# Layer-0 attention: value products grouped by six key tiles, wider maxima with a shift row written by DMA, column-tiled sums

## The chip, the core and the metric

The kernel runs on one core of a Trainium2 chip. Its work is spread over TensorE (PE; its weight loads are shown as PEld), VectorE (DVE), ScalarE (ACT), GpSimd (POOL) and SyncE (SP, which here issues nearly all DMAs). The metric is device time in microseconds of one execution, lower is better; three executions of the kernel before the change took 2945.24, 2954.23 and 2960.78 us.

## The reference

A backbone of two layers over 2048 tokens and 256 context tokens. Layer 0 has a convolution beside a grouped-query attention (8 heads of 64, 2 key heads, keys of context and tokens together, so 2304), layer 1 a Fourier mixing beside a neighbourhood attention. Only the attention of layer 0 is touched by the change:

```python
def dense_attn(q, k, v):
    Bq, Lq, Hq, dh = q.shape
    Hk = k.shape[2]
    qg = q.reshape(Bq, Lq, Hk, Hq // Hk, dh)
    s = jnp.einsum('bqkgd,bskd->bkgqs', qg, k).astype(jnp.float32) * (dh ** -0.5)
    p = jax.nn.softmax(s, axis=-1).astype(v.dtype)
    o = jnp.einsum('bkgqs,bskd->bqkgd', p, v)
    return o.reshape(Bq, Lq, Hq * dh)
...
    y_b = blocked_attn(q, jnp.concatenate([ck, k], axis=1), jnp.concatenate([cv, v], axis=1))
    y_a = conformer_conv(a_val, a_gate, conv_w, conv_b, ln_g, ln_b)
    y = jnp.concatenate([y_a, y_b], axis=-1) * jax.nn.silu(z)
    x = x + gate * (y @ w_out)
    if need_ctx:
        cq = rms_norm(uc[..., AB_Q_OFF:AB_K_OFF].reshape(Bx, L, B_HEADS, HEAD_DIM), qn_g)
        yc_b = dense_attn(cq, ck, cv)
```

For a query the context attends to the 256 context keys only, the tokens to all 2304.

## The kernel before

The stages follow each other: input projection and convolution of layer 0, this attention (`ab_attention`), the output projection of layer 0, then the same for layer 1. In the profiled execution the attention lies between about 735 and 1600 us.

**Units and steps.** The attention works in units: two heads of one group for 256 queries, so 512 query columns. 32 units (token queries) have 18 tiles of 128 keys, 4 units (context queries, put in at indices 0, 4, 8 and 12) have 2. A step of the schedule is one key tile of one unit, 584 in all; `first` is the step at which a unit starts. Scores stand with the keys on partitions. They are negated, and high and low halves of queries and keys are kept apart: a score is two products, `s<-q,k0h` (high and low query on the high keys) and `s<-qm,k0l` (high query on the low keys, with further rows below that carry the shift).

**Maxima, a unit ahead.** So that no exponential overflows, each query's greatest score is taken off. `chunk` (line 854) computes scores again in one pass, with the queries on partitions: five products of up to 512 keys for each of four groups of 128 queries, 16 of 512 keys and 4 of 256 in a unit, each reduced by DVE from one of three PSUM buffers `m` (line 864). `least` joins the five columns, and `shift_row` (line 870) transposes the result on PE, and DVE (line 874) spreads it over four rows of the contraction of `qm`, one for each 128 queries. This is done 7 steps (`AHEAD`) or more ahead of the unit; a chunk falls on each 0.85 of a step.

**Scores, exponentials, values.** `score` (line 881) puts its two products into one of two PSUM buffers `s`; ACT's exponential (line 890) writes `pr`, of which there are six. Every second step, three steps (`LAG`) later, `multiply` (line 893) does the value products of two tiles (line 900): they are plain float32, each with 64 output columns, one in the upper and one in the lower half of the array, so that the two run side by side; the trace records each as two instructions, so a pair of tiles shows as x4. `add` sums the exponentials over the tiles, 7 tiles on DVE (`accd`), 11 on POOL (`accp`).

**A unit's end.** `unload` copies the values out of PSUM on ACT. Then a chain with fixed distances (`CHAIN`) from the last step of the unit: `join` adds both sums on POOL, `sum_high` (ACT) and `sum_low` (DVE) split them, `total` (line 950, tile `row`) sums over the partitions with two products into one row, which ACT copies to `srow` (line 956); SP puts it on 128 partitions (`rc`, line 958), `invert` takes reciprocals on DVE (line 964), two DMAs (lines 965, 967) bring them by way of DRAM to all partitions (`r`); `divide` (POOL, line 971), `fold` (ACT, two copies) and `store` (POOL, line 983, and a DMA) follow. The pool `rp` holds one buffer each of `srow`, `sh`, `sl` and `r`.

**What sets the order.** `at(step, order, f)` notes what each step does; the loop at the end of `ab_attention` emits it step by step, in the order of the second number, under `manual_schedule`, which keeps this order on PE, ACT, DVE and POOL. Each engine works its own list in that order and stands where the next entry isn't ready. The DMAs on SP aren't under that order; the framework's scheduler places them. `extra` puts in the background work by step: the modulation's columns of both layers (`ada_part`, 512 KB loads and small products, up to about step 130), the patterns of layer 1's attention bias (DMAs), and from step 220 the convolution's norm.

## Time and profile before

| | us |
|---|---|
| median of three runs | 2954.23 |
| lowest, highest run | 2945.24, 2960.78 |
| span of the profiled execution, first to last instruction | 2944.6 |
| attention, first score to last value product | 836 |
| PE, DVE, POOL, ACT busy in the whole span | 2764.9, 1855.9, 1531.5, 1134.3 |

The page gives the profiled execution's span, and no time outside it; the span is just under the lowest timed run. An engine's busy time is the union of its instructions' records. The records of PE overlap, since a product drains while the next one streams in, so the time a product costs is read from start to start, not from its length. In a row of the timeline stand start, length, engine, line, operation, output<-inputs, the shape and the count; in brackets the idle time ahead of it and what ended it.

### The profile page before, as it was taken

To read this page: it belongs to the slowest core of one execution; us is meant where nothing else is said; L and a number is where in the kernel's file an instruction comes from. 1 tells how busy PE (TensorE), PEld (TensorE's weight loads), DVE (VectorE), ACT (ScalarE), POOL (GpSimd) and SP (SyncE) were. 2 spreads that over 40 slices of the span, in tenths; PEclk is the share of its full clock that TensorE was granted. 3 is DMA by queue.
4 is the path that set the end of the run, shared out by engine and by line. 5 is a ranking of instruction groups with operands and counts; after the bars stand their busy time and mean duration, and the time that the engine had idled before them with its cause. 6 is when DMAs were issued, how large, how long until landed. Compare 5 with 4: busy or idle time off the path is not lost.

```text
span 2944.6 us, 40977 instructions
## 1 busy us (share of the span) xinstructions
PE 2764.9 (94%) x14481; PEld 2128.3 (72%) x14481; DVE 1855.9 (63%) x2867; ACT 1134.3 (39%) x2103; POOL 1531.5 (52%) x1173
## 2 busy tenths in 40 slices
PE   7988799986999999999999999999999997998998
PEld 5988799886444444444445887988898886888787
DVE  4798869896877788888887564101211336777663
ACT  3223131320354555555554223123222335777421
POOL 3568624846465788778785754222122312455343
PEclk9999899998999999999999999999999998999999
DMA  8224131361642343331123653433333349999852
GB/s 249 91 77 147 53 106 47 96 179 36 196 136 78 123 138 101 90 121 55 51 63 106 235 166 136 150 127 106 126 140 128 111 152 238 220 246 225 273 197 89
DMA packets 345752, 397.66 MB, mean 135 GB/s; under 512 B 54844, under 2 KB 270444, under 8 KB 340555
## 3 DMA queue, kind: packets, MB, share of 16 engines
q1 hardware_dynamic: 344971, 390.85, 44.9%
q10 hardware_dynamic: 576, 4.19, 0.4%
q8 instruction: 114, 1.87, 0.3%
q14 instruction: 91, 0.75, 0.1%
HBM read 270.34 MB, written 129.78 MB: 136 GB/s over the span
## 4 chain that ended last, share of the span: by engine, by line
PE 65%; DMA 11%; DVE 9%; POOL 6%; issue 4%; ACT 1%; SPq 0%; POOLq 0%; ACTq 0%; DVEq 0%
PE av L900 9%; PE s L885 9%; PE mm L415 7%; PE mm L417 7%; PE mm L416 7%; PE m L862 6%; DVE acc L517 5%; DMA nv<-v_d 4%; POOL wlo L431 4%; PE mo L1087 3%; PE mo L1086 3%; PE mo L1085 3%; DMA nk<-k 3%; PE mm L424 2%; PE mm L426 1%
## 5 line engine op out<-in xcount | busy, mean ns | idle before, releaser
L431 POOL TENSOR_TENSOR wlo<-wraw,whi 128x1024 fp32r<-128x1024 f32 x86 | 323.8, 3774 | 499.7 <-ACT whi L430 481.1
L864 DVE TENSOR_REDUCE ast<-m 128x1 f32<-128x512 f32 (+1 forms) x656 | 398.7, 626 | 176.8 <-PE m L862 174.5
L890 ACT ACTIVATE pr<-s 128x512 f32<-128x512 f32 x584 | 343.1, 595 | 298.6 <-PE s L885 253.9
L925 POOL TENSOR_TENSOR accp<-accp,pr 128x512 f32<-128x512 f32 x283 | 398.7, 1409 | 88.1 <-ACT pr L890 74.2
L517 DVE SCALAR_TENSOR_TENSOR acc<-u,cw,acc 128x1151 f32<-128x1151 f32 (+1 forms) x240 | 366.5, 1582 | 0.0
L900 PE MATMUL av<-pr,vt 128*64 128x512 f32 x1168 | 317.4, 622 | 0.0
L417 PE MATMUL mm<-hi_ab,wlo 128*128 128x384 f32 x768 | 260.6, 341 | 39.1 <-POOL wlo L431 39.1
L415 PE MATMUL mm<-hi_ab,whi 128*128 128x384 f32 x768 | 261.0, 346 | 11.6 <-DVE qraw L729 7.2
L416 PE MATMUL mm<-lo_ab,whi 128*128 128x384 f32 x768 | 261.7, 342 | 0.0
L415 PE MATMUL mm<-hi_cd,whi 128*128 128x512 f32 x640 | 250.8, 392 | 1.1 <-ACT hi_cd L379 1.1
L416 PE MATMUL mm<-lo_cd,whi 128*128 128x512 f32 x640 | 250.1, 391 | 0.4 <-DVE lo_cd L380 0.4
L417 PE MATMUL mm<-hi_cd,wlo 128*128 128x512 f32 x640 | 246.7, 390 | 0.0
L417 PEld LDWEIGHTS mm<-hi_ab,wlo 128*128 128x128 f32 x768 | 147.5, 192 | 39.8 <-POOL wlo L431 39.8
L925 DVE TENSOR_TENSOR accd<-accd,pr 128x512 f32<-128x512 f32 x165 | 165.7, 1004 | 0.9 <-ACT pr L890 0.5
L1642 DVE TENSOR_TENSOR nlo<-npt,nhi 128x512 fp32r<-128x512 f32 x192 | 123.6, 644 | 62.1 <-ACT nhi L1640 61.4
L862 PEld LDWEIGHTS m<-k1h,q 128*128 128x128 f32 x328 | 62.2, 190 | 132.9 <-DVE ast L864 84.9
L415 PEld LDWEIGHTS mm<-hi_ab,whi 128*128 128x128 f32 x768 | 147.5, 193 | 14.1 <-DVE qraw L729 7.6
L1604 POOL TENSOR_SCALAR npr<-npr,nst 128x640 f32<-128x640 f32 (+1 forms) x128 | 108.1, 858 | 89.8 <-DVE nst L1603 66.7
L371 DVE TENSOR_SCALAR ht<-ptr,scale,shift 128x384 f32<-128x384 f32 (+2 forms) x96 | 61.2, 671 | 147.4 <-PE ptr L368 146.7
L862 PEld LDWEIGHTS m<-k0h,q 128*128 128x128 f32 x328 | 63.3, 195 | 125.0 <-DVE ast L864 80.6
L430 ACT ACTIVATE whi<-wraw 128x1024 fp32r<-128x1024 f32 x88 | 92.9, 1059 | 148.3 <-PE mm L416 135.5
L416 PEld LDWEIGHTS mm<-lo_ab,whi 128*128 128x128 f32 x768 | 147.8, 193 | 0.8 <-DVE lo_ab L380 0.8
(321 smaller groups left out, 7002.1 us busy)
## 6 DMA issues: line engine op xcount, KB each, us to landing
wraw<-in_cd_w_in_dram SPq DMA_DIRECT2D x46, 512.0 KB, 4.0
wraw<-in_ab_w_in_dram SPq DMA_DIRECT2D x42, 512.0 KB, 3.5
pat_d<-big SPq DMA_DIRECT2D x72, 256.0 KB, 3.7
nk<-k SPq DMA_DIRECT2D x32, 576.0 KB, 12.7
pat<-pat_d SPq DMA_DIRECT2D x24, 768.0 KB, 6.5
nv<-v_d SPq DMA_DIRECT2D x128, 128.0 KB, 7.0
adaraw<-in_ab_w_ada_dram SPq DMA_DIRECT2D x24, 512.0 KB, 6.1
adaraw<-in_cd_w_ada_dram SPq DMA_DIRECT2D x24, 512.0 KB, 3.7
```

What stands on the lines that cost most here:

```text
L415: nc.tensor.matmul(ps, a, hh[:, k, cols], start=k == 0, stop=False)
L416: nc.tensor.matmul(ps, a, hl[:, k, cols], start=False, stop=False)
L417: nc.tensor.matmul(ps, b, hh[:, k, cols], start=False, stop=k == KT - 1)
L431: (eng or nc.vector).tensor_tensor(out=lo, in0=src, in1=hi.bitcast(F32), op=ALU.subtract)
L517: ins = nc.vector.scalar_tensor_tensor(out=acc[:, :n], in0=u[:, tap : tap + n], scalar=cw[:, ch, tap : tap + 1], in1=acc[:, :n], op0=ALU.m ...
L862: nc.tensor.matmul(ps[:, :n], lhs, kt[hp // 2][0][:, a : a + n], start=True, stop=True)
L864: nc.vector.tensor_reduce(out=s["st"][:, qt, col : col + 1], in_=ps[:, :n], axis=AX.X, op=ALU.min)
L885: nc.tensor.matmul(ps[:], kt[hp // 2][key][:, k * P : k * P + P], s[x][:].rearrange("p j n -> p (j n)"), start=key == 0, stop=key == 1,)
L890: nc.scalar.activation(pr[:], ps[:], AF.Exp, scale=-1.0)
L900: nc.tensor.matmul(s["av"][x * 64 : x * 64 + 64], vt[:, k - 1 + x, kv * 64 : kv * 64 + 64], s["pr"][k - 1 + x][:], start=k == 1, stop=k == ...
L925: eng.tensor_tensor(out=s[name][:], in0=first_in[:], in1=s["pr"][k][:], op=ALU.add)
L1642: return lambda: nc.vector.tensor_tensor(out=lo[:, :o], in0=pt[:, :o], in1=hi[:, :o].bitcast(F32), op=ALU.subtract)
```

## The change

- Value products are done in groups of six tiles, at steps 5, 11 and 17 of a unit (a unit of two tiles: at its second step), straight behind that step's score and chunk. `pr` has nine buffers.
- A chunk covers 1024 keys of 128 queries: two products into a PSUM tile of two banks, one reduction by DVE. The last 256 keys of all four groups of queries go together. Nine chunks in a unit, every second step. `m` has two such tiles.
- The shift is one row of the contraction in place of four. DVE negates the maxima into `sr` (queries on partitions), and four DMAs, 128 elements of 4 bytes each, write them into row 64 of `qm`. The transpose and DVE's spreading go.
- `join`, `sum_high` and `sum_low` go. `total` sums `accd` and `accp` by two float32 products in two column halves, into one of the two buffers of `s`, behind the first group of value products that ends at least five steps after the unit. `spread` copies rows 0 to 64 on ACT and sends two rows to `rc`; `invert` adds them before the reciprocal. The last unit sums with full-width float32 products.
- DVE takes the tiles 4, 5, 10, 11, 15, 16, 17, and adds them at the step of their group's value products; POOL's additions come one step after the score, not two.
- The other differences of the diff are comments and docstrings left out.

```diff
-            lo = kp.tile([68, T], F32R, name=f"k{kv}l")
+            lo = kp.tile([65, T], F32R, name=f"k{kv}l")
...
-            tp = self.pool(es, "apt", 6)
+            tp = self.pool(es, "apt", 9)
...
-            ps_m = self.pool(es, "psm", 3, PSUM)
+            ps_m = self.pool(es, "psm", 2, PSUM)
             ps_s = self.pool(es, "pss", 2, PSUM)
             ps_a = self.pool(es, "psa", 1, PSUM)
-            ps_r = self.pool(es, "psr", 1, PSUM)
             ps_c = self.pool(es, "psc", 1, PSUM)
             self.inv_d = [self.dram(f"inv{a}", [1, 512]) for a in range(2)]
-            onesr = rp.tile([P, P], F32R, name="onesr")
-            nc.vector.tensor_copy(onesr[:], self.ones[:])
-            AHEAD, LAG, SUM, RATE, ROW = 7, 3, 2, 0.85, 4
+            AHEAD, SUM, RATE, GROUP = 7, 1, 2, 6
...
-            CHAIN = (5, 7, 9, 11, 14, 19, 21, 22)
+            CHAIN = (1, 4, 9, 11, 12)
...
-            def chunk(i, qt, c):
+            def chunk(i, c):
                 b, hp = units[i]
                 s = state[i]
-                a = c * 512
-                n = min(512, tiles[i] * P - a)
-                lhs = s["q"][:, qt // 2, (qt % 2) * P : (qt % 2) * P + P]
-                ps = ps_m.tile([P, 512], F32, name="m", tag="m")
-                nc.tensor.matmul(ps[:, :n], lhs, kt[hp // 2][0][:, a : a + n], start=True, stop=True)
-                col = c if b else 5
-                nc.vector.tensor_reduce(out=s["st"][:, qt, col : col + 1], in_=ps[:, :n], axis=AX.X, op=ALU.min)
-
-            def least(i):
-                st = state[i]["st"]
-                nc.vector.tensor_reduce(out=st[:, :, 5:6], in_=st[:, :, 0:5], axis=AX.X, op=ALU.min)
+                ps = ps_m.tile([P, 1024], F32, name="m", tag="m")
+                key = kt[hp // 2][0]
+                if b and c < 8:
+                    parts = [(c // 2, c % 2 * 1024 + x * 512, 512) for x in range(2)]
+                else:
+                    parts = [(qt, 2048 if b else 0, 256) for qt in range(4)]
+                for x, (qt, a, n) in enumerate(parts):
+                    lhs = s["q"][:, qt // 2, (qt % 2) * P : (qt % 2) * P + P]
+                    nc.tensor.matmul(ps[:, x * n : x * n + n], lhs, key[:, a : a + n], start=True, stop=True)
+                if len(parts) == 2:
+                    nc.vector.tensor_reduce(
+                        out=s["st"][:, c // 2, c % 2 : c % 2 + 1], in_=ps[:], axis=AX.X, op=ALU.min
+                    )
+                else:
+                    nc.vector.tensor_reduce(
+                        out=s["st"][:, :, 2 if b else 3], in_=ps[:].rearrange("p (q n) -> p q n", q=4), axis=AX.X, op=ALU.min
+                    )
 
             def shift_row(i):
                 s = state[i]
-                pt = ps_r.tile([P, 512], F32, name="row", tag="row")
-                nc.tensor.transpose(pt[0:4, 0:P], s["st"][:, :, 5], self.ident[:])
-                nc.vector.scalar_tensor_tensor(
-                    out=s["qm"][64:68].rearrange("p j (i n) -> p (j i) n", n=P),
-                    in0=pt[0:4, 0:P].unsqueeze(1).broadcast_to((4, 4, P)), scalar=-1.0,
-                    in1=self.ident[0:4, 0:4].unsqueeze(2).broadcast_to((4, 4, P)), op0=ALU.mult, op1=ALU.mult,
-                )
+                st = s["st"]
+                if units[i][0]:
+                    nc.vector.tensor_reduce(out=st[:, :, 3:4], in_=st[:, :, 0:3], axis=AX.X, op=ALU.min)
+                row = sp.tile([P, 4], F32R, name="sr", tag="sr")
+                nc.vector.tensor_scalar(out=row[:], in0=st[:, :, 3], scalar1=-1.0, scalar2=None, op0=ALU.mult)
+                for qt in range(4):
+                    to = s["qm"][64:65, qt // 2, (qt % 2) * P : (qt % 2) * P + P].bitcast(F32)
+                    nc.sync.dma_start(to.rearrange("o (n f) -> o n f", f=1), row[:, qt : qt + 1].bitcast(F32))
...
-            def multiply(i, k):
+            def multiply(i, first_k, n):
                 b, hp = units[i]
                 s = state[i]
-                if k == 1:
+                if first_k == 0:
                     s["av"] = ps_a.tile([P, 512], F32, name="av", tag="av")
                 kv = hp // 2
-                for x in range(2):
+                for k in range(first_k, first_k + n):
+                    x = k % 2
                     nc.tensor.matmul(
-                        s["av"][x * 64 : x * 64 + 64], vt[:, k - 1 + x, kv * 64 : kv * 64 + 64], s["pr"][k - 1 + x][:],
-                        start=k == 1, stop=k == tiles[i] - 1,
+                        s["av"][x * 64 : x * 64 + 64], vt[:, k, kv * 64 : kv * 64 + 64], s["pr"][k][:],
+                        start=k < 2, stop=k >= tiles[i] - 2,
                     )
...
+            def by_dve(i):
+                return [4, 5, 10, 11, 15, 16, 17] if i < len(units) - 1 else list(range(TAIL, NT))
             def add(i, k):
                 s = state[i]
-                n = tiles[i]
-                if n == 2:
-                    mine, eng, name = [0, 1], nc.vector, "accd"
-                else:
-                    dve = [3 * x + 2 for x in range(5)] + [16, 17] if i < len(units) - 1 else list(range(TAIL, n))
-                    mine, eng, name = (dve, nc.vector, "accd") if k in dve else ([x for x in range(n) if x not in dve], nc.gpsimd, "accp")
+                if tiles[i] == 2:
+                    s["accd" if k == 0 else "accp"] = s["pr"][k]
+                    return
+                dve = by_dve(i)
+                mine, eng, name = (dve, nc.vector, "accd") if k in dve else ([x for x in range(NT) if x not in dve], nc.gpsimd, "accp")
...
-            def join(i):
+            def total(i):
                 s = state[i]
-                if "accp" in s:
-                    nc.gpsimd.tensor_tensor(out=s["accd"][:], in0=s["accd"][:], in1=s["accp"][:], op=ALU.add)
-
-            def sum_high(i):
-                s = state[i]
-                s["sh"] = rp.tile([P, 512], F32R, name="sh", tag="sh")
-                nc.scalar.activation(s["sh"][:], s["accd"][:], AF.Copy)
-
-            def sum_low(i):
-                s = state[i]
-                s["sl"] = rp.tile([P, 512], F32R, name="sl", tag="sl")
-                nc.vector.tensor_tensor(
-                    out=s["sl"][:], in0=s["accd"][:], in1=s["sh"][:].bitcast(F32), op=ALU.subtract
-                )
-
-            def total(i):
-                s = state[i]
-                pt = ps_r.tile([P, 512], F32, name="row", tag="row")
-                m = 1 if i < len(units) - 1 else P
-                for x in ("sh", "sl"):
-                    nc.tensor.matmul(pt[0:m], onesr[:, 0:m], s[x][:], start=x == "sh", stop=x == "sl")
-                if m == P:
+                pt = s["tot"] = ps_s.tile([P, 512], F32, name="s", tag="s")
+                if i == len(units) - 1:
+                    for x in ("accp", "accd"):
+                        nc.tensor.matmul(pt[:], self.ones[:], s[x][:], start=x == "accp", stop=x == "accd")
                     s["r"] = rp.tile([P, 512], F32, name="r", tag="r")
                     nc.vector.reciprocal(s["r"][:], pt[:])
                     return
-                row = rp.tile([1, 512], F32, name="srow", tag="srow")
-                nc.scalar.activation(row[:], pt[0:1], AF.Copy)
-                s["rc"] = sp.tile([P, 4], F32, name="rc", tag="rc")
-                nc.sync.dma_start(s["rc"][:], row[0:1].rearrange("o (p f) -> o p f", f=4))
+                for x, name in enumerate(("accd", "accp")):
+                    nc.tensor.matmul(pt[x * 64 : x * 64 + 64], self.ones[:, 0:64], s[name][:], start=True, stop=True)
+            def spread(i):
+                s = state[i]
+                if "r" in s:
+                    return
+                row = rp.tile([65, 512], F32, name="srow", tag="srow")
+                nc.scalar.activation(row[:], s["tot"][0:65], AF.Copy)
+                s["rc"] = sp.tile([P, 2, 4], F32, name="rc", tag="rc")
+                for x in range(2):
+                    nc.sync.dma_start(s["rc"][:, x], row[64 * x : 64 * x + 1].rearrange("o (p f) -> o p f", f=4))
 
             def invert(i):
                 s = state[i]
                 if "r" in s:
                     return
-                nc.vector.reciprocal(s["rc"][:], s["rc"][:])
-                nc.sync.dma_start(self.inv_d[i % 2].rearrange("o (p f) -> (o p) f", f=4), s["rc"][:])
+                rc = s["rc"]
+                nc.vector.tensor_tensor(out=rc[:, 0], in0=rc[:, 0], in1=rc[:, 1], op=ALU.add)
+                nc.vector.reciprocal(rc[:, 0], rc[:, 0])
+                nc.sync.dma_start(self.inv_d[i % 2].rearrange("o (p f) -> (o p) f", f=4), rc[:, 0])
...
-                chunks = [(qt, c) for qt in range(4) for c in range(5 if units[i][0] else 1)]
+                n = 9 if units[i][0] else 1
                 time = min(time - RATE, first[i] - AHEAD)
-                last = int(time // 1)
-                for x in reversed(chunks):
-                    at(int(time // 1), 4, bind(chunk, i, *x))
-                    begin = int(time // 1)
-                    time -= RATE
-                time += RATE
+                last = time
+                for x in reversed(range(n)):
+                    begin = time = last - RATE * (n - 1 - x)
+                    at(time, 3, bind(chunk, i, x))
                 at(begin - 3, 0, bind(load_q, i))
                 at(last - 2, 0, bind(load_high, i))
-                if units[i][0]:
-                    at(last + 1, 5, bind(least, i))
-                at(last + ROW, 1, bind(shift_row, i))
+                at(last, 5, bind(shift_row, i))
+            bursts = [first[i] + k for i, n in enumerate(tiles) for k in range(n) if k % GROUP == GROUP - 1 or k == n - 1]
             for i, n in enumerate(tiles):
                 for k in range(n):
                     s = first[i] + k
                     at(s, 2, bind(score, i, k))
-                    if k % 2 == 1:
-                        at(s + LAG + 0, 3, bind(multiply, i, k))
-                    at(s + SUM, 6, bind(add, i, k))
+                    end = min(k // GROUP * GROUP + GROUP, n)
+                    if k == end - 1:
+                        at(s, 4, bind(multiply, i, k // GROUP * GROUP, end - k // GROUP * GROUP))
+                    late = k in by_dve(i) and i < len(units) - 1
+                    at(first[i] + end - 1 if late else s + SUM, 6, bind(add, i, k))
                 e = first[i] + n - 1
-                at(e + LAG, 4, bind(unload, i))
-                ds = {len(units) - 2: CHAIN[:5] + (22, 24, 25), len(units) - 1: (2, 4, 4, 8, 8, 9, 10, 11)}.get(i, CHAIN)
-                for d, f in zip(ds, (join, sum_high, sum_low, total, invert, divide, fold, store)):
-                    at(e + d, 7, bind(f, i))
+                at(e + 1, 1, bind(unload, i))
+                t = min([x for x in bursts if x >= e + 5], default=e + 2)
+                at(t, 7, bind(total, i))
+                ds = CHAIN if i < len(units) - 1 else (0, 0, 1, 2, 3)
+                for d, f in zip(ds, (spread, invert, divide, fold, store)):
+                    at(t + d, 8 if t + d == t else 1, bind(f, i))
```

8 lines of the change are left out of this document (4 added, 4 removed).

## The prediction

> **What bounds the kernel now.** I read the page's head first, then the chain that ended last, then the stretch of the attention.
>
> ```profile
> span 2944.6 us, 40977 instructions
> ...
> PE 2764.9 (94%) x14481; PEld 2128.3 (72%) x14481; DVE 1855.9 (63%) x2867; ACT 1134.3 (39%) x2103; POOL 1531.5 (52%) x1173
> ...
> PE 65%; DMA 11%; DVE 9%; POOL 6%; issue 4%; ACT 1%; SPq 0%; POOLq 0%; ACTq 0%; DVEq 0%
> ```
>
> PE leads. The busy times of the stretch from the first score to the last value product:
>
> ```profile
> 752.00:1588.00 836.00, 819.20 (x3403) 388.25 (x3403) 674.76 (x1033) 447.56 (x803) 617.49 (x474) 0.99 0.33 97
> ```
>
> The columns after the length are PE, PEld, DVE, ACT, POOL, granted clock, DMA share. 836 us carry 584 steps (one key tile each: 32 units of 18, 4 units of 2), 1.43 us a step, and PE is busy in 98%. A busy PE may still lose time between its products, so the PE timeline decides; the time of a product is the distance to the next start:
>
> ```profile
> 937.65 0.40 PE L862 MATMUL m<-k0h,q 128*128 128x512 f32 x1
> 937.89 0.40 PE L885 MATMUL s<-q,k0h 128*128 128x512 f32 x1
> 938.12 0.40 PE L885 MATMUL s<-qm,k0l 68*128 68x512 f32 x1
> 938.45 1.08 PE L900 MATMUL av<-pr,vt 128*64 128x512 f32 x4
> 939.46 0.49 PE L862 MATMUL m<-k0h,q 128*128 128x512 f32 x1
> 939.80 0.40 PE L950 MATMUL row<-sh,onesr 128*1 128x512 f32 x1
> 940.03 0.39 PE L950 MATMUL row<-sl,onesr 128*1 128x512 f32 x1
> ```
>
> A score or maximum product costs 0.23 (937.65 to 937.89). The one ahead of the value products takes 0.33 and the one behind them 0.34: the change of kind costs 0.10 on each side. The value products of two tiles take 1.01 between. So a pair alone costs 1.21 us, and there is no gap to blame: the attention is bound by PE's own queue. Near the end the trace has two pairs together:
>
> ```profile
> 1585.48 0.39 PE L885 MATMUL s<-qm,k1l 68*128 68x512 f32 x1
> 1585.80 1.94 PE L900 MATMUL av<-pr,vt 128*64 128x512 f32 x8
> 1587.66 0.49 PE L1121 MATMUL pl<-mean_w,sm 128*128 128x1 f32 x3
> ```
>
> 1.86 us for both: the second pair costs 0.85 where a lone one costs 1.21.
>
> **The change part by part.** *Bursts.* A unit of 18 tiles goes from nine lone pairs to three bursts of three: 1.21 + 2 x 0.85 = 2.91 instead of 3.63, 0.72 a burst, 96 bursts: **-69**. This rests on one place; were a later pair 1.01, only the edges went: 192 x 0.20 = -38.
>
> *Sums.* Before: two products in fp32r, 0.23 each. After: two fp32 column tiles behind a burst, as one more value pair, 0.85. 35 x (0.85 - 0.46): **+14**. Join (POOL), high (ACT) and low (DVE) part go, with PE's wait for them:
>
> ```profile
> PEld row L950 <- DVE sl L940: 11.6, 8, 3.3
> ...
> PE row L950 <- DVE sl L940: 7.5, 6, 2.7
> ```
>
> PE stood 7.5 us (PEld's time lies mostly under other products), and one of these stands brought a half-speed stretch of 1.7 (below): **-9**. The small transposes of the shift rows (L873) I take as nothing.
>
> *Maxima.* The products stay. DVE's reductions go from 16 and 4 a unit to 9 of 1024:
>
> ```profile
> L864 DVE TENSOR_REDUCE ast<-m 128x1 f32<-128x512 f32 x495 | 332.0, 685 | 117.1 <-PE m L862 115.0
> ...
> L864 DVE TENSOR_REDUCE ast<-m 128x1 f32<-128x256 f32 x136 | 56.7, 418 | 29.8 <-PE m L862 29.6
> ```
>
> 256 more elements cost 0.27, so 1024 cost about 1.22 (at most 2 x 0.685): 11.0 us a unit instead of 12.6. DVE is not the bound (675 of 836) and its in-order work has cover; I take 0, bounds -5 and +10. The additions that DVE now makes at a burst's end, and POOL a step earlier, have the nine `pr` buffers as cover: exponential k+9 needs tile k's burst and addition, which lie three steps back or more; an addition over 2 us late would hold ACT.
>
> *ACT between bursts.* Steps without value products take PE 0.46 and half of 0.46, 0.69. Two PSUM buffers of scores remain, so ACT's round trip must keep up:
>
> ```profile
> 1101.51 0.39 PE L885 MATMUL s<-qm,k0l 68*128 68x512 f32 x1
> ...
> 1101.94 0.60 ACT L890 ACTIVATE pr<-s 128x512 f32<-128x512 f32 x1 [0.20 <-PE s L885]
> ```
>
> ```profile
> 859.30 0.59 ACT L956 ACTIVATE srow<-row 1x512 f32<-1x512 f32 x1 [3.19 <-DMA rc<-srow]
> 859.80 1.05 ACT L890 ACTIVATE pr<-s 128x512 f32<-128x512 f32 x2
> ```
>
> ```profile
> 860.42 0.50 PE L885 MATMUL s<-q,k0h 128*128 128x512 f32 x1 [0.22 <-ACT pr L890]
> ```
>
> First product 0.23, then 0.43 to the exponential, 0.60 for it, 0.02 to 0.05 back: 1.3 us for two steps against PE's 1.38. It just fits; nothing is left for an ACT instruction that waits. The sums now take one of those two buffers until ACT has copied them out (0.1 + 0.59): the second score behind the burst waits 0.3 instead of starting at 0.46. 32 x 0.3: **+10**.
>
> *Two totals in one burst.* Three small units lie between large ones; the sums of the large unit before and of the small one both fall due at step 5 of the next unit (before, two steps apart). `srow` and `r` have one buffer each. What that costs before:
>
> ```profile
> 855.07 0.51 SPq L958 DMA_DIRECT2D rc<-srow  x1
> ...
> 859.92 0.50 SPq L958 DMA_DIRECT2D rc<-srow  x1
> 860.90 0.34 SPq L967 DMA_DIRECT2D r<-inv  x1
> ...
> 866.21 0.32 SPq L967 DMA_DIRECT2D r<-inv  x1
> ```
>
> ```profile
> 864.91 1.27 POOL L971 TENSOR_TENSOR o<-o,r 128x512 f32<-128x512 f32 x1 [0.94 <-DMA r<-inv]
> ...
> 869.76 1.28 POOL L971 TENSOR_TENSOR o<-o,r 128x512 f32<-128x512 f32 x1 [2.35 <-DMA r<-inv]
> ```
>
> The second `srow` waited on ACT for the first one's transfer (3.19 above); the second `r` went out when the first division ended (866.2), and the second division started 3.6 us later. After, both copies stand side by side in ACT's queue ahead of the exponentials, and both folds too. The second copy starts 0.7 + 0.5 + 2.0 = 3.2 us after the burst and frees a score buffer at 4.0: PE stands 3.5. The second division ends 3.6 + 1.3 = 4.9 us after the first, its fold (0.85) behind it, and exponentials 16 and 17 behind that; the burst of step 17 can run 1.9 us without them: I take 5.5 us. 3 x 9: **+27** (bounds 0 and 36).
>
> *Clock.* After a stand PE runs slow:
>
> ```profile
> 1473.68 0.40 PE L950 MATMUL row<-sh,onesr 128*1 128x512 f32 x1
> 1476.79 0.49 PE L950 MATMUL row<-sl,onesr 128*1 128x512 f32 x1 [2.72 <-DVE sl L940]
> ```
>
> ```profile
> 1476.80:1480.50 3.70, 3.70 (x10) 1.70 (x10) 2.07 (x4) 1.78 (x3) 3.62 (x3) 0.54 0.34 107
> ```
>
> 3.1 us of standing, then 3.7 us at a granted 0.54: 1.7 us lost. Six stands: **+10**. The Trainium skill ("TensorE: Matmul & The Clock Gate", Part 1) has the half clock come after one idle window of about 3.4 us, and has the windows run free; by the page a stand of 3.5 would seldom cover one, and the sum would be 5 lower. This trace speaks against that, with 3.1 us enough.
>
> *Reciprocals and fold.* With one total, `r` comes by
>
> ```profile
> r<-inv SPq DMA_DIRECT2D x35, 256.0 KB, 4.1
> ...
> rc<-srow SPq DMA_DIRECT2D x35, 2.0 KB, 2.0
> inv<-rc SPq DMA_DIRECT2D x35, 2.0 KB, 1.4
> ```
>
> 0.7 for the copy, 0.5 for the second of the two issues, 2.0, 0.4 on DVE, 1.4, 4.1: 9.1 us after the burst. POOL gets to the division (step 14) after burst 2 (4.4 + 2.9), the exponential of step 12 (1.3) and its own addition:
>
> ```profile
> L925 POOL TENSOR_TENSOR accp<-accp,pr 128x512 f32<-128x512 f32 x268 | 378.9, 1414 | 79.0 <-ACT pr L890 65.6
> ```
>
> that is, at about 10.0. Division and fold end at 12.2, exponential 17 at 13.4, when the third burst's last pair wants it (7.3 + 4.1 + 1.9 = 13.3). Even; 0.2 a unit: **+6** (0 and 40).
>
> *Shift rows.* Four DMAs of 128 elements of 4 bytes replace transpose and DVE's 0.68. The score's second product now waits for SP; the exponentials, and with them all of PE, queue behind it. From the last chunk (step 11) to that score lie two bursts and six steps, 10 us. Spent: reduction 1.2 to 2.4, row 0.3, four issues of 0.5 and, by the nearest row (`rc`), 2.0: 5.5 to 6.7. Hidden by 3 us; SP, which gets five more issues of 0.5 a unit, has sent `inv` and `r` by then (5.0 after the first burst, where the rows are due at 6.5). I take 0, bounds 0 and +20.
>
> *Ends.* Fewer reductions ahead of the first score -3; no join, high and low at the end -4; 25 last steps without maxima are paced by ACT +2: **-5**.
>
> Sum: -69 + 14 - 9 + 10 + 27 + 10 + 6 - 5 = **-16 us**. The profiled span lies 0.6 under the lowest run (2945.24); the median is 2954.23, and I take the difference from it: **2938 us**, -0.5%.
>
> **Rivals.** (a) *The buffers cost nothing*: PE's stands at paired totals, clock and copies are covered: -69 + 14 - 9 + 6 - 5 = -63, 2891. For: the pairing existed before and cost PE 0.2 us there (860.42). Against: that was with two steps between. (b) *Slower: the fold becomes the bound.* If `r` lands 1.5 us later than I sum, each unit's exponentials 16 and 17 hold the third burst 1.5 us: 32 x 1.5 = 48 on top, +32 or 2986; it turns the sign from 0.5 us a unit (16 / 32). For: 4.1 is a median, and DMA is a third busy. Against: POOL is itself no earlier than 10.0. (c) *Shift rows late*: beside the modulation's 512 KB loads, first seven units, 3 us each: +21 on top, 2959. The Trainium skill ("DMA: Bandwidth & Descriptors", Specifications) says writes under 512 B are read, modified and written. No run here shows the price for 4 bytes; a doubled landing would just use up the 3 us. (d) *The burst doesn't save inside*: -38 for -69: +15, 2969.
>
> **Numbers.** Forecast, 2920 to 2955: 0.47. (a) 0.23, (b) 0.13, (c) 0.09, (d) 0.08. 2890 to 2974 leaves out about half of (a) and most of (b), 0.2. Faster by over 0.5% (14.8 us, about what a measurement of this kernel can tell from no change; under 2939.5): (a) and a good half of the forecast, 0.50. Slower (over 2969): (b) and half of (d), 0.16. Same: 0.34.
>
> **What would show it.** Right: value products in groups of twelve at about 2.7 us and the next start, one PE wait for `srow` at each sum, six stands of 3 to 6 us with the clock at half behind them in the first third. Wrong: PE waiting in every unit for exponential 17 (b), for `qm` from DMA (c), or for DVE's reductions; twelve products over 3.0 us (d). If PE waits nowhere, (a).

## The result and the profile after

The changed kernel takes 2997.2 us (median of 4 runs, 2992.27 to 3004.64), the one before 2957.4 beside it (4 runs, 2945.24 to 2960.78): ratio 1.0139, 95% interval 1.0114 to 1.0164, slower by 41 us by this ratio (the medians differ by 39.8). 2938 was forecast. The page's head of the changed kernel, span, busy times and the chain that ended last:

```profile
span 2990.2 us, 40866 instructions
...
PE 2755.5 (92%) x14517; PEld 2153.5 (72%) x14517; DVE 1788.9 (60%) x2497; ACT 1106.7 (37%) x2067; POOL 1480.5 (50%) x1141
...
PE 60%; DMA 13%; DVE 8%; POOL 7%; issue 5%; ACT 2%; SPq 1%; POOLq 0%; ACTq 0%; DVEq 0%
```

PE, DVE, ACT and POOL are all busy for less time than before (PE 2764.9 then; only its weight loads, PEld, take more, 2128.3 then), and the span is 45.6 us longer: time went into waits. The first row below is the stretch of the attention (length; PE, PEld, DVE, ACT, POOL; granted clock, DMA share, GB/s), the second its first 84 us:

```profile
752.00:1613.00 861.00, 805.87 (x3440) 410.90 (x3440) 612.58 (x686) 420.86 (x769) 567.39 (x449) 0.98 0.35 98
752.00:836.00 84.00, 73.26 (x328) 37.62 (x329) 45.33 (x57) 35.20 (x64) 39.40 (x33) 0.92 0.54 153
```

PE was busy in 819 of 836 us before and is in 806 of 861 now: 13 less busy time, 55 without work instead of 17. To see more than busy time shows, I took all starts of PE's products from the traces, from the first score to the last value product. A product's time is the distance to the next start, up to 0.345 us for scores and maxima, 0.545 for value products and sums, 0.44 for the rest; what is beyond counts as a stand (at half clock, a part of a product's own time too). Half clock is the time, within the length, at which the trace grants half:

```
us             length  score  maxima  value  sums  other  stands | half clock
before          834.7  308.8   162.1  294.9  19.2   27.1    23.1 |  14.5
after           859.6  314.0   142.3  276.1  33.2   28.6    65.8 |  40.3
sums apart      835.6  314.0   141.9  272.8  34.6   28.1    44.7 |  25.4
 + row on chip  830.7  313.5   141.7  273.4  35.0   29.2    38.4 |  13.9
 + third buffer 810.5  295.1   146.6  274.4  34.9   27.9    32.6 |  11.8
 + bursts late  805.7  292.8   148.8  267.7  33.5   28.1    35.2 |  14.2
```

(The lower four are experiments.) Maxima and value products fell, scores rose by 5.2 and sums by 14.0, and the stands grew by 42.7. Two kinds of place hold 34 of the 65.8 us of stands: the paired sums (23.5) and the first large unit (10.3). A third loss, short waits at score products, lies below the bound and thus in the scores' column. **Paired sums**, PE's timeline after the small units; the bracket is the wait ahead of a product:

```profile
862.91 0.39 PE L889 MATMUL s<-qm,k0l 65*128 65x512 f32 x1
865.85 0.49 PE L889 MATMUL s<-q,k0h 128*128 128x512 f32 x1 [2.55 <-ACT srow L954]
```

```profile
880.14 1.94 PE L906 MATMUL av<-pr,vt 128*64 128x512 f32 x8
888.88 2.46 PE L906 MATMUL av<-pr,vt 128*64 128x512 f32 x4 [6.80 <-ACT pr L894]
```

In the upper rows PE waits for the second copy. In the lower ones eight value products of a burst run in 1.94, and its last four start at 888.88. ACT's second copy, then ACT, POOL and SP ahead of 888.88:

```profile
865.20 0.59 ACT L954 ACTIVATE srow<-s 65x512 f32<-65x512 f32 x1 [2.75 <-DMA rc<-srow]
```

```profile
887.35 0.41 ACT L977 ACTIVATE yb<-o 64x256 f32<-64x256 f32 x1 [6.75 <-POOL o L972]
```

```profile
886.06 1.26 POOL L972 TENSOR_TENSOR o<-o,r 128x512 f32<-128x512 f32 x1 [6.34 <-DMA r<-inv]
```

```profile
876.58 4.62 SPq L275 DMA_DIRECT2D toep<-rp  x4
881.29 0.85 SPq L968 DMA_DIRECT2D r<-inv  x1
```

Read backwards: value product, exponential, fold (887.35), second division (886.06), broadcast of `r`, which SP sends at 881.29. The one buffer `r` was free from 879.7 on, when the first division (started at 878.44) ended; until 881.2 four other DMAs stood ahead on SP. The three places cost 2.94 + 7.39, 3.00 + 3.68 and 2.96 + 6.16 = 26 us from start to start (23.5 beyond the table's bound).

**The first large unit**, PE, then DVE and SP:

```profile
757.50 0.50 PE L889 MATMUL s<-q,k0h 128*128 128x512 f32 x1
768.12 0.77 PE L889 MATMUL s<-qm,k0l 65*128 65x512 f32 x1 [10.12 <-DMA q<-qs]
```

```profile
752.09 0.17 DVE L879 TENSOR_SCALAR sr<-ast 128x4 fp32r<-128x4 f32 x1
```

```profile
759.10 0.92 SPq L226 DMA_DIRECT2D adaraw<-in_cd_w_ada_dram  x2
760.12 2.84 SPq L882 DMA_DIRECT2D qm<-sr  x4
```

The row stands ready at 752.26. SP sends it from 760.12 on, behind loads of the modulation's weights, and the score that reads it starts at 768.12. (The page names `q<-qs`, which was sent earlier; the product reads `qm`, and PEld's own wait there is for `qm<-sr`.) What follows runs at half clock:

```profile
768.20:772.00 3.80, 3.80 (x9) 3.03 (x10) 1.23 (x1) 1.72 (x3) 1.27 (x1) 0.50 0.91 295
```

This unit takes 36.4 us instead of 24.2. **Short waits**, too small for my bound of a stand, lie at the first product of each score (groups by line: busy, mean ns of one | idle before):

```profile
L889 PE MATMUL s<-q,k0h 128*128 128x512 f32 x292 | 133.5, 457 | 8.5 <-ACT srow L954 7.7 <-ACT pr L894 0.2
L889 PE MATMUL s<-q,k1h 128*128 128x512 f32 x292 | 131.0, 449 | 5.3 <-ACT pr L894 4.4
```

The same groups of the kernel before:

```profile
L885 PE MATMUL s<-q,k0h 128*128 128x512 f32 x292 | 120.8, 414 | 1.8 <-ACT pr L890 1.8
L885 PE MATMUL s<-q,k1h 128*128 128x512 f32 x292 | 119.8, 410 | 3.5 <-ACT pr L890 3.5
```

The mean rose by about 40 ns, although fewer changes of kind lie beside scores now. In PE's timeline such a product starts 0.24 after the one before it and the next only 0.31 later:

```profile
1106.41 0.40 PE L889 MATMUL s<-qm,k0l 65*128 65x512 f32 x1
1106.65 0.47 PE L889 MATMUL s<-q,k0h 128*128 128x512 f32 x1
1106.96 0.39 PE L889 MATMUL s<-qm,k0l 65*128 65x512 f32 x1
...
1107.77 2.80 PE L906 MATMUL av<-pr,vt 128*64 128x512 f32 x12
1110.49 0.50 PE L889 MATMUL s<-q,k0h 128*128 128x512 f32 x1
```

The row of twelve is a burst: 2.72 to the next start, as the two pairs of the prediction promised. Over the whole attention, at full clock, a recorded value product takes 234 ns, so 2.81 for twelve.

### The profile page after: what moved, and what is told of

It is laid out like the page before. It is cut to its first block, busy times and chain, and to the rows that moved or that the text cites. A ratio compares the mean times of both kernels' runs of the same rounds, so it can differ in the third digit from the quotient of the medians.

```text
span 2990.2 us, 40866 instructions
## 1 busy us (share of the span) xinstructions
PE 2755.5 (92%) x14517; PEld 2153.5 (72%) x14517; DVE 1788.9 (60%) x2497; ACT 1106.7 (37%) x2067; POOL 1480.5 (50%) x1141
## 4 chain that ended last, share of the span: by engine, by line
PE 60%; DMA 13%; DVE 8%; POOL 7%; issue 5%; ACT 2%; SPq 1%; POOLq 0%; ACTq 0%; DVEq 0%
PE s L889 8%; PE av L906 8%; PE mm L415 6%; PE mm L417 6%; PE mm L416 6%; DVE acc L517 4%; POOL wlo L431 3%; PE mo L1087 3%; PE m L863 3%; PE mo L1088 3%; PE mo L1089 3%; DMA nv<-v_d 3%; DMA nk<-k 3%; PE mm L424 2%; PE mm L426 2%
## 5 line engine op out<-in xcount | busy, mean ns | idle before, releaser
L933 POOL TENSOR_TENSOR accp<-accp,pr 128x512 f32<-128x512 f32 x283 | 379.4, 1341 | 194.1 <-ACT pr L894 177.2
L865 DVE TENSOR_REDUCE ast<-m 128x1 f32<-128x1024 f32 x256 | 308.6, 1217 | 189.4 <-PE m L863 188.9
L894 ACT ACTIVATE pr<-s 128x512 f32<-128x512 f32 x584 | 328.8, 596 | 207.4 <-PE s L889 195.4
L906 PE MATMUL av<-pr,vt 128*64 128x512 f32 x1168 | 289.3, 609 | 23.0 <-ACT pr L894 22.8
L906 PEld LDWEIGHTS av<-pr,vt 128*64 128x64 f32 x1168 | 79.5, 137 | 172.8 <-issue 119.5
L889 PE MATMUL s<-q,k0h 128*128 128x512 f32 x292 | 133.5, 457 | 8.5 <-ACT srow L954 7.7
```

Of the source, the lines that this page charges most:

```text
L865: nc.vector.tensor_reduce(out=s["st"][:, c // 2, c % 2 : c % 2 + 1], in_=ps[:], axis=AX.X, op=ALU.min)
L889: nc.tensor.matmul(ps[:], kt[hp // 2][key][:, k * P : k * P + P], s[x][:].rearrange("p j n -> p (j n)"), start=key == 0, stop=key == 1,)
L894: nc.scalar.activation(pr[:], ps[:], AF.Exp, scale=-1.0)
L906: nc.tensor.matmul(s["av"][x * 64 : x * 64 + 64], vt[:, k, kv * 64 : kv * 64 + 64], s["pr"][k][:], start=k < 2, stop=k >= tiles[i] - 2,)
L933: eng.tensor_tensor(out=s[name][:], in0=first_in[:], in1=s["pr"][k][:], op=ALU.add)
```

## The experiments

Not all ran on one chip; each ratio is against runs of the kernel before on the same chip (their medians lie between 2957.0 and 2960.2 us), and gains between experiments are differences of these ratios times 2958, each uncertain by 8 to 13 us. "Length" is that of the attention in the table's sense.

### Sums apart

The sums of a large unit ahead of a small one are taken in the small unit's own burst, two steps behind the last score, so that no burst holds two.

```diff
-                t = min([x for x in bursts if x >= e + 5], default=e + 2)
+                wait = 2 if i + 1 < len(units) and tiles[i + 1] == 2 else 5
+                t = min([x for x in bursts if x >= e + wait], default=e + 2)
```

> The changed kernel, but the sums of a large unit that stands before a small one are taken in the small unit's own burst (two steps after the large unit's end), so that no burst carries two sums. Theory 'paired sums' (three bursts with two sums wait for the single srow and the single r buffer): the six stands of PE of 2.9 to 7.4 us (26 us in the trace) and the half-clock stretches behind them go, 28 to 38 us less than the changed kernel, ratio to before about 1.002 to 1.006. Rival 'spread loss' (each unit loses a little to ACT or POOL, the stands are covered by later slack): under 8 us less, ratio 1.011 or more.

2966.41 us, ratio 1.0028 (1.0009 to 1.0047): 33 us of the 41 are gone. The units behind the small ones fall from 39.6, 36.6 and 34.9 us to 29.0, 28.1 and 24.4 (29.5, 29.6 and 25.7 in the kernel before), stands from 65.8 to 44.7, half clock from 40.3 to 25.4; the attention is 24.0 shorter. The paired sums are the largest single cost.

### The row from ACT's queue, alone and together

The shift rows of the first two units are sent by ACT instead of SP, to leave SP's order; once in the changed kernel, once with the sums apart.

```diff
-                    nc.sync.dma_start(to.rearrange("o (n f) -> o n f", f=1), row[:, qt : qt + 1].bitcast(F32))
+                    eng = nc.scalar if i < 2 else nc.sync
+                    eng.dma_start(to.rearrange("o (n f) -> o n f", f=1), row[:, qt : qt + 1].bitcast(F32))
```

> The changed kernel, but the shift rows of the first two units are sent from ACT's queue, not SP's. Theory 'row behind loads' (the first large unit's shift row is sent 8 us late on SP, behind the modulation's loads, and lands 5 us later still): the stand of 10.6 us at the first large unit goes for the most part, 8 to 15 us less than the changed kernel with the half clock. Rival (the landing, not the sending, is what is slow, because the 16 engines are full of the loads): 0 to 5 us less, the score's second product still waits 5 us or more.

> Both edits together. If both theories hold they add: 38 to 50 us less than the changed kernel, ratio to before 0.996 to 1.002. If the loss is spread over all units: ratio 1.008 or more.

2992.09 us, ratio 1.0126 (1.0099 to 1.0153), and 2966.92, ratio 1.0034 (1.002 to 1.0048): 4 us less than the changed kernel, inside the noise, and nothing beside the sums apart. The stand only moved. ACT in the first of the two kernels:

```profile
739.99 26.04 ACTq L883 DMA_DIRECT2D qm<-sr  x8
766.06 1.28 ACT L895 ACT_TABLE_LOAD   x1 [29.44 <-DMA qm<-sr]
```

Eight sends of about 0.5 us each held ACT's queue for 26 us. The second row was ready at 753.66 and its four sends start at 759.98, 760.50, 763.58 and 765.55, with nothing else on that queue. The DMA engines were full:

```profile
752.00:766.00 14.00, 4.90 (x10) 2.88 (x10) 5.04 (x6) 0.00 (x0) 0.00 (x0) 0.62 1.08 301
```

So SP's order is not the whole cause: beside the loads (301 GB/s) a small DMA is late from either queue, and on ACT it holds up the exponentials as well.

What holds the sends stands in the trace, though in none of the views shown. A DMA reports its landing on a semaphore. This program has eight of them for its 1843 DMAs, handed out in turn over both queues (230 or 231 each), and a DMA is not sent before the one eight places earlier, which has the same semaphore, has landed (in 1816 of 1835 such pairs the trace has all 16 landings of the one ahead of the next send; in the rest it records fewer). Of the eight sends on ACT, five start 0.02 us after that landing (741.34, 745.74, 749.35, 763.56, 765.53), and one, at 759.98, 0.08 after it; the landings at 745.74, 763.56 and 765.53 are those of 512 KB loads that SP had sent 5.9, 7.6 and 6.2 us earlier. In the changed kernel the loads ahead of the row on SP wait in the same way: the sends at 757.07 and 759.10 start 0.02 us after such landings. The row's data then takes 5.1 us from the end of its last send (762.96) to land (768.03).

### The row on the chip again

In the kernel with the sums apart, transpose and VectorE write as before the change (four rows of the contraction), two steps behind the last maximum.

```diff
-                for qt in range(4):
-                    to = s["qm"][64:65, qt // 2, (qt % 2) * P : (qt % 2) * P + P].bitcast(F32)
-                    nc.sync.dma_start(to.rearrange("o (n f) -> o n f", f=1), row[:, qt : qt + 1].bitcast(F32))
+            def spread_row(i):
+                pt = ps_m.tile([P, 1024], F32, name="m", tag="m")
+                nc.tensor.transpose(pt[0:4, 0:P], s["st"][:, :, 3], self.ident[:])
+...
+                at(last + 2, 1, bind(spread_row, i))
```

> The kernel with the sums apart (2966.4 us), and in it the shift row put in again by a TensorE transpose and one VectorE write of four rows, two steps after the unit's last maximum, in place of the four DMAs. Theory 'the row waits behind the loads': the first large unit falls from about 37.7 us to about 25, its wait of some 10 us and the half clock after it go, all other units stay as they are or grow by the price of one transpose each (0.2 to 0.4 us, 36 units, 7 to 14 us, mostly in place of waits): 2952 to 2962 us, ratio 0.998 to 1.002. Rival 'the first unit is late for another reason (its maxima are not done in time)': its length stays near 37 us and the time at 2966 or above, since the transposes only add: 2966 to 2980.

2955.61 us, ratio 0.9982 (0.9961 to 1.0002), 14 us less than with the sums apart. The first large unit falls from 37.7 to 24.8, and half clock from 25.4 to 13.9, about its value of before. In this profile the attention as a whole is only 4.9 shorter, since 8 us come back in other units: transposes, and maxima behind them, now wait for DVE, 9 us in ten stands. PE at the place of the stand runs through:

```profile
757.64 2.45 PE L911 MATMUL av<-pr,vt 128*64 128x512 f32 x4 [0.32 <-ACT pr L899]
760.03 0.80 PE L894 MATMUL s<-q,k0h 128*128 128x512 f32 x1
760.62 0.63 PE L894 MATMUL s<-qm,k0l 68*128 68x512 f32 x1
```

### The row by DMA alone

The reverse: the kernel before, and in it only the shift row by four DMAs (`shift_row` as in the change), sent right behind the maxima; then the same with division, fold and store three steps later.

```diff
-                at(last + ROW, 1, bind(shift_row, i))
+                at(last + 1, 5, bind(shift_row, i))
```

```diff
-            CHAIN = (5, 7, 9, 11, 14, 19, 21, 22)
+            CHAIN = (5, 7, 9, 11, 14, 22, 24, 25)
```

> The kernel before, and in it the shift row alone by four DMAs of 128 values right after the maxima (step 'least'), in place of transpose, VectorE write and three further rows. Theory 'only the first large unit's row comes late': 10 to 15 us longer in that unit and nothing in the other units, less the 36 transposes (0.1 to 0.3 us each): 2957 + 0 to 12, ratio 1.000 to 1.004. Rival 'the rows are late at the large units after small ones too': units after small ones grow by 3 us or more, ratio 1.006 or more. Rival 'the DMA row is hidden': first large unit stays at 24 to 26 us and the time at 2945 to 2957.

> The kernel before with the shift row by four DMAs (2998.0 us), and in it the division three steps later (22 steps after the unit's last score in place of 19), and with it fold and store (24 and 25). Theory 'the row's four sends stand in SP's queue ahead of the broadcast of the reciprocals, the division comes late, ScalarE waits at the fold, and score products wait for ScalarE': ScalarE's waits for the division (32.6 us) go, about 20 us: 2973 to 2983 us, ratio 1.004 to 1.008, the first large unit still at about 40 us. Rival 'the row itself is late in many units': no change, 2993 to 3003 us.

The row alone: 2998.03 us, ratio 1.0108 (1.0067 to 1.0149), so none of the three expectations holds. The ratio is in the range of the second (1.006 or more), but the units behind small ones grew by 1.5, 0.0 and 1.4, not by 3. The first large unit grew by 16.5 (24.2 to 40.7), a little more than the first expectation had, but the attention by 36.6, the rest scattered over other units. There PE stands behind ACT, ACT behind POOL's division, POOL behind `r`. The waits of the whole span (total, times, longest):

```profile
POOL o L969 <- DMA r<-inv: 127.1, 31, 8.1
...
PEld s L883 <- ACT pr L888: 35.6, 41, 4.3
...
ACT yb L974 <- POOL o L969: 32.6, 21, 5.8
```

The same waits in the kernel before:

```profile
POOL o L971 <- DMA r<-inv: 78.7, 31, 3.8
...
PEld s L885 <- ACT pr L890: 14.7, 16, 2.9
...
ACT yb L976 <- POOL o L971: 8.1, 2, 7.4
```

One such place in the kernel with the row by DMA, SP and PE:

```profile
1068.53 0.53 SPq L956 DMA_DIRECT2D rc<-srow  x1
1072.38 2.45 SPq L876 DMA_DIRECT2D qm<-sr  x4
1074.88 2.10 SPq L275 DMA_DIRECT2D pat_d<-big  x4
1077.07 0.59 SPq L963 DMA_DIRECT2D inv<-rc  x1
```

```profile
1087.42 0.80 PE L883 MATMUL s<-q,k0h 128*128 128x512 f32 x1 [4.02 <-ACT pr L888]
```

SP stands until the row is ready (1072.36), then sends it. DVE's reciprocals ended at 1074.3; their way out waits on SP behind the four row sends and four pattern DMAs. From `rc` to `inv` lie 8.5 us here and 4.2 in the kernel before (1050.45 to 1054.69); 2.7 of the difference lie on SP, the rest ahead of the reciprocals. With the division three steps later: 2965.84 us, ratio 1.0016 (0.9998 to 1.0033), 27 us less, more than the 20 expected; the attention is 27.2 shorter. The same waits:

```profile
POOL o L969 <- DMA r<-inv: 21.6, 13, 4.0
...
ACT yb L974 <- POOL o L969: 7.8, 4, 6.6
```

The first large unit still takes 40.7. The row by DMA has thus two prices: one late landing beside the loads, and four sends ahead of a chain in SP's queue. In the changed kernel the division stands 9 steps behind the sums (8 in the kernel before, 11 here). Once its sums are apart, the second price hardly shows: value products wait 10.7 us for ACT with the row by DMA and 9.1 with the row on the chip.

### A third buffer of scores

First, with sums apart and the row from ACT: maxima in two tiles of 512 in one step, with three buffers for them, which leaves room for a third score buffer. Then, with the row on the chip, the maxima as 18 pieces of 512, one in each step, and again three and three (RATE is changed in this one alone).

```diff
-            ps_m = self.pool(es, "psm", 2, PSUM)
-            ps_s = self.pool(es, "pss", 2, PSUM)
+            ps_m = self.pool(es, "psm", 3, PSUM)
+            ps_s = self.pool(es, "pss", 3, PSUM)
...
-            AHEAD, SUM, RATE, GROUP = 7, 1, 2, 6
+            AHEAD, SUM, RATE, GROUP = 7, 1, 1, 6
...
-                ps = ps_m.tile([P, 1024], F32, name="m", tag="m")
+                ps = ps_m.tile([P, 512], F32, name="m", tag="m")
```

> Both edits, and the maxima again in tiles of 512 (three PSUM banks), which leaves a third score buffer. Theory 'round trip' (with two score buffers the products wait 0.05 to 0.1 us for ACT all along, 24 us in the attention, and 0.3 us at each sum): 15 to 30 us less than with both edits alone, ratio to before 0.985 to 0.995. Rival 'order' (the short waits are PE's own switch costs, not the buffers): within 5 us of both edits alone, or slower by DVE's 12.6 against 11.0 us a unit.

> Sums apart, shift row by transpose, and the maxima as 18 pieces of 512 keys, one a step, in three buffers, which frees a bank for a third score buffer. Theory 'with a third buffer the short waits go, and one piece of 512 a step does not make the maxima wait for VectorE': against the kernel with the transpose alone score products about 19 us shorter and no waits between two maxima (they were 36 us where two came back to back): 2930 to 2945 us, ratio 0.990 to 0.996. Rival 'VectorE's 512-key reductions are the limit wherever they stand (18 of them against 9 larger ones a unit)': waits of maxima on VectorE of 15 us and more stay, 2955 to 2985 us.

The first: 2984.13 us, ratio 1.0104 (1.0079 to 1.0129), 21 us more than the kernel it is built on, where 15 to 30 less was expected. Scores fall from 313.0 to 294.0, so the short waits were the two buffers'; but 36 us of stands between two maxima of one step came instead. The second maximum of a step now waits for DVE:

```profile
L893 PE MATMUL s<-q,k0h 128*128 128x512 f32 x292 | 125.9, 431 | 0.0
...
L865 PE MATMUL m<-k1h,q 128*128 128x512 f32 (+1 forms) x328 | 100.3, 380 | 24.6 <-DVE ast L868 24.6
```

The second: 2944.62 us, ratio 0.9937 (0.9913 to 0.9961), faster than both kernels. Scores stay at 295.1, and stands between two maxima are gone. But maxima behind a score still wait for DVE, 15 us by the table's bound: the rival's sign is there, though the time is the theory's. A unit without a stand takes 22.4 us, where with two buffers it took 23.0.

### Pairs again

Value products in pairs, two steps behind their second score, once with two score buffers (sums apart), once with three.

```diff
-                    if k == end - 1:
-                        at(s, 4, bind(multiply, i, k // GROUP * GROUP, end - k // GROUP * GROUP))
+                    if k % 2 == 1:
+                        at(s + 2, 3.5, bind(multiply, i, k - 1, 2))
...
-                at(e + 1, 1, bind(unload, i))
+                at(e + 2, 4, bind(unload, i))
```

> The kernel with the sums apart (2966.4 us), and in it the value products in pairs again, each two steps after its second score, in place of bursts of six. Theory 'the bursts save, and the two score buffers take a part back': the changes of form come back in 24 large-unit places and more (score, maxima and value products together about 57 us longer), the short waits of score products on ScalarE go (about 24 us shorter): 2966 + 33 = about 2999 us, 2988 to 3010, ratio 1.010 to 1.018, with score products that start 0.23 us after the one before instead of 0.25 to 0.31. Rival 'the bursts save nothing in this kernel': 2960 to 2972, no change.

> The kernel with three buffers of scores (2944.6 us), and in it the value products in pairs again, two steps after their second score, in place of bursts. Theory 'the bursts' saving is real at about 60 us where no score product waits for a buffer, and two buffers hid half of it': more than the 29 us that the same undoing cost with two buffers: 2944.6 + 45 to 65 = 2990 to 3010 us, ratio 1.010 to 1.017. Rival 'the saving is about 30 us whatever the buffers': 2965 to 2980 us, ratio 1.002 to 1.007.

```
us                     all   length  score  maxima  value  stands  unit without a stand
two buffers, bursts  2966.4   835.6  314.0   141.9  272.8    44.7         23.0
two buffers, pairs   2995.6   851.5  316.7   157.3  291.8    24.9         24.65
three, bursts        2944.6   810.5  295.1   146.6  274.4    32.6         22.4
three, pairs         2958.9   830.1  311.5   160.3  291.2     6.1         24.4
```

Ratios of the two with pairs: 1.0093 (1.0062 to 1.0124) and 1.0002 (0.9983 to 1.0021), so that the bursts are worth 19 us with two buffers and 19 with three (15.9 and 19.6 in the attention's length), give or take 11 and 9. With two, the time is in the expected range, the ratio just under it. The score column did not fall (316.7), yet the short waits went: a third buffer takes 18.4 us off the scores with bursts (313.5 to 295.1), but only 5.2 with pairs (316.7 to 311.5); the changes of kind came back in their place. With three, both expectations missed in size; a gain that differs with the buffers is not seen within this noise. The table says why it is small. With three buffers a unit without a stand gains 2.0 and the products of all units 47, but the stands give back 26.5. They lie at the bursts' ends (value products) and at maxima. Three buffers, bursts, then pairs:

```profile
L912 PE MATMUL av<-pr,vt 128*64 128x512 f32 x1168 | 288.4, 606 | 10.0 <-ACT pr L900 9.9
...
L863 PE MATMUL m<-k1h,q 128*128 128x512 f32 (+1 forms) x328 | 119.1, 381 | 12.9 <-DVE ast L865 12.6
```

```profile
L912 PE MATMUL av<-pr,vt 128*64 128x512 f32 x1168 | 315.0, 617 | 0.0
...
L863 PE MATMUL m<-k1h,q 128*128 128x512 f32 (+1 forms) x328 | 116.4, 373 | 2.6 <-DVE ast L865 2.5
```

### Bursts one step later

With three buffers, each burst (not the last unit's) one step later, so that its last exponential has a step's time; the sums, which stand behind a burst, move with it.

```diff
-                        at(s, 4, bind(multiply, i, k // GROUP * GROUP, end - k // GROUP * GROUP))
+                        at(s + (i < len(units) - 1), 4, bind(multiply, i, k // GROUP * GROUP, end - k // GROUP * GROUP))
...
-                at(e + 1, 1, bind(unload, i))
+                at(e + 1, 4.5 if i < len(units) - 1 else 1, bind(unload, i))
```

> The kernel with three buffers of scores and bursts (2944.6 us), and in it each burst one step later (but for the last unit), after the score and the maximum of the next step, so that the exponential of its last tile need not be ready at once. Theory 'a good part of what the bursts save goes back in stands at the burst's own end: value products wait 10 us for ScalarE's last exponential': these stands shrink to 2 us or less, 2930 to 2941 us, ratio 0.988 to 0.993 against before. Rival 'the bursts' loss is VectorE's (maxima waiting for reductions that stand behind the late additions, 15 us)': 2941 to 2950 us, the stands of maxima remain.

2930.36 us, ratio 0.9906 (0.9882 to 0.993): 28 us faster than the kernel before, and the lowest of all (9 us below the one with the bursts in place, though the two intervals overlap). The value products' wait shrinks, that of the maxima grows:

```profile
L912 PE MATMUL av<-pr,vt 128*64 128x512 f32 x1168 | 280.0, 605 | 3.5 <-ACT pr L900 3.5
...
L863 PE MATMUL m<-k1h,q 128*128 128x512 f32 (+1 forms) x328 | 120.7, 386 | 18.0 <-DVE ast L865 17.6
```

The stands as a whole did not shrink (32.6 to 35.2): the attention is 4.8 us shorter, and the value products' column fell by 6.7, which points to short waits inside the bursts. Both kinds of stand are there, and DVE's is what is left.

### The kernel before, profiled again

> The kernel before unchanged, for a second profile. Theory 'the stretch of layer 1 that shows 11 to 16 us more in the profiles of all changed kernels was short by chance in the one profile of before': a span of 2950 to 2960 us with the attention at 833 to 837 us and the additional 6 to 14 us after 2440 us. Rival 'the changed attention moves layer 1': a span of 2943 to 2947 us again and the stretch as short as in the first profile.

A span of 2958.8 us instead of 2944.6, with the attention at 837.4, and 1359.8 instead of 1348.2 from its last value product to PE's last product. The first profile is a short execution: its span lies under the lowest of all timed runs of this kernel (2945.24). Of the 20 us that the changed kernel's profile shows more behind the attention (1368.2), 11.6 are the luck of that profile. In the other kernels this part takes 1356 to 1378, with one and the same code from the output projection on. Of the 8 us that are left, 2 are seen at the attention's end: the first product of the output projection starts 3.0 us behind the last value product, 1.0 in the kernel before. The rest was not traced. All ten profiles with the new sums have 1360 to 1378 here and the four without 1348 to 1365, so it need not be scatter alone.

## Why the prediction was wrong

By terms, against the first profile of before; "product columns" are score, maxima and value, and the last row but one goes to PE's last product:

```
us                                    predicted   measured
bursts, clock (product columns)         -69 +10      -33.4
sums (their column)                         +14      +14.0
stands: sl, score buffer, pairs, fold     +35.5      +42.7
other products                                0       +1.5
ahead of the first score                     -3       +0.5
behind the last value product                -4      +20.0
sum                                         -16      +45.3
```

(The stands predicted: 7.5 off, 10 + 27 + 6 on; of the -9 for `sl` the other 1.7 was clock, and of the ends the last 25 steps' +2 lies in no row. The profiles' spans differ by 45.6. By the products that start at half clock, against the mean of the others, half clock costs about 7 us more than before: 4.6 in the product columns, 2.6 in the stands. So the bursts are worth about 38 where 69 was forecast.)

**Right in mechanism and nearly in size.** *Two totals in one burst*: +27 and most of the clock's +10 were predicted, with the copy behind the transfer and the second division behind `r`; the stands are 26 us (10.3, 6.7 and 9.1 for my 9 each), and moving the sums gave back 33. *Sums*: 33.2 against 19.2, and +0.4 in a unit of pairs with three buffers, 24.4 against 24.0. *Reciprocals and fold*: +6 (0 to 40); with the sums apart, value products wait 10.7 us for ACT in 11 places, and ahead of each of the four longest ACT does a fold for which it had waited for POOL's division. It is the small form of rival (b). *Inside of a burst*: where nothing waits, the second and third pair cost what the one place near the end had shown: 2.72 for six tiles and 0.2 for both edges, 2.92 for my 2.91; the mean is 0.09 more. Rival (d), over 3.0, is out. *Maxima*: 1217 ns for the reduction, 1.22 estimated.

**Wrong: "It just fits".** PE's 1.38 against ACT's 1.3 for two steps left 0.08, and I booked only the sums' copy (+10). A unit without a stand should have taken 24.0 - 2.16 + 0.39 + 0.3 = 22.53 and takes 23.03: 0.5 a unit, which I estimate as 16 us for 32 units, in waits of up to about 0.08 that no list of waits shows as a stand. A third buffer takes them away (scores 313.0 to 294.0, units to 22.4). The step took a short round trip for the usual one. From a score's first product to the end of its exponential I had 1.26; in the changed kernel the median of all 584 is 1.37, and in 95 of 100 cases at least 0.07 more passes until the next product in that buffer: 1.44 against PE's 1.38.

**Wrong: "Hidden by 3 us".** Shift rows were taken at 0 (0 to +20). The 2.0 for landing came from `rc`, a median of 35 places, most of them without the modulation's loads beside them. (Nor would a doubled landing have used up the 3 us: 2.0 more would have left 1.3 by the sum.) In the first large unit 8 us passed until SP sent the row and 5.2 from the last send (762.96) to the score: that unit took 12 us longer, and the row on the chip gave 14 back. Rival (c) had the cause, but spread over seven units at 3 us each instead of one at 12. I had counted the queue SP only by its issues, five of 0.5 a unit, and not by what stood in front of them, nor by the landings that each send waits for.

**Wrong: where the bursts' gain goes.** Of the -69, the product columns show about 38 with two buffers and 47 with three; it would be 2.0 x 32 = 64 if every unit were like those without a stand. But a burst asks for its last exponential at once, and maxima wait for DVE. That DVE's additions stand in a heap in front of them can't be the whole cause: they stand at the same steps in the kernel with pairs and three buffers, where maxima hardly wait (2.5 us for `k1h`, 12.6 with bursts). What fits, but was not tested, is the pace: between bursts a step takes PE 0.69, and DVE's reduction of 512 keys alone takes 0.685. I had the first as the fold's +6 and gave the second a bound of +10 at "maxima". With three buffers the stands rose by 26.5, and the whole gained 19 us.

**Wrong: ends.** -5 was forecast. The first score came 0.5 later, not 3 earlier; the last unit took 31.6 instead of 27.2 (forecast +2; with the third buffer 24.8), with 6.8 us of half clock and a product of the convolution's norm (`pl<-mean_w,sm`) that stood 2.8 for POOL. The output projection began 2.0 later behind the last value product, not 4 earlier. What lies behind that differs by 11.6 between two profiles of one kernel, and I made the sum against the shorter of the two.

The sign came from these together: about 16 for short waits, 12 for the first unit, 12 for the ends (3.5 ahead, 2.4 in the last unit, 6 behind it), and the rest of the 57 between forecast and ratio, about 17, in stands at bursts and maxima, in bursts of 2.81 instead of 2.72, and in scatter; this last part I cannot split further.

On the clock I had set the trace against the Trainium skill ("TensorE: Matmul & The Clock Gate", Part 1), whose one idle window of about 3.4 us would seldom fit into a stand of 3.5. The runs don't side with my "3.1 us is enough" throughout: the stand of 2.94 ahead of 865.85 and that of 3.68 ahead of 982.85 brought no half clock; those of 3.00 and 2.96 at the other two paired sums (ahead of 962.05 and 1048.01) and those of 6.2, 7.4 and 10.6 did.

## What to carry to other kernels

A round trip through two buffers that "just fits" should be booked as a small wait in every step, and looked for in the mean duration of the waiting product, since lists of waits hardly show it. A transfer of some bytes is as late as the queue in front of it and the load beside it: take its price at the place where it will run, ask which chain's DMAs are sent behind it on the same queue, and look which earlier DMA each send waits for. Work put together in bursts gains at its edges, but is due all at once: move the burst a step behind its last input, and look at the pace that it leaves to the other engines between bursts.

## What was not expected of the hardware

- Sends of 512 bytes took 26 us for eight on an otherwise empty ACT queue while the DMA engines moved 275 to 301 GB/s, since six of them waited for the landing of the DMA eight places earlier, SP's loads among them; sent without such loads (1 GB/s from 1072 to 1075), four took 2.45 us on SP.
- The length of a stand doesn't decide alone whether the clock halves. In the changed kernel PE stood 2.94 us (862.91 to 865.85) and ran on at full clock; in the kernel before it stood 2.03 (1320.12 to 1322.15), ran four products 0.23 to 0.34 apart, and then fell to half:

```profile
865.80:869.30 3.50, 3.45 (x26) 2.19 (x27) 2.18 (x4) 1.70 (x4) 2.72 (x3) 1.00 0.30 39
```

```profile
1323.20:1327.00 3.80, 3.80 (x10) 1.14 (x9) 1.30 (x3) 0.92 (x2) 3.56 (x4) 0.55 0.06 20
```

- Two profiles of the same kernel differ by 14 us in span, 11.6 of them behind the attention, with the DMA engines 95% busy in both from 2440 to 2850 us, in layer 1.
